# The query projection of a decoder block as a Strassen step, with streamed weight sums

## The chip, the cores and the metric

The kernel runs on one core of a Trainium2 chip. Its engines work beside one another, each with its own list of instructions, done in order: TensorE (PE in the profile; PEld is its loading of weights), VectorE (DVE), ScalarE (ACT), GpSimd (POOL) and SyncE (SP), whose list here is nearly all of the kernel's DMA issues. The metric is the device time of one execution in microseconds (us).

## The reference

One decoder block on `x` of 1024 tokens by 1024 features, in fp32. A mixer with two branches comes first, then cross-attention to 256 memory tokens (4 heads of 256), then a SwiGLU network with 2816 inner features. The change touches the middle:

```
merged = sigmoid(g_ssd) * (y_ssd @ w_up_ssd) + sigmoid(g_gla) * (y_gla @ w_up_gla)
h = x + merged @ w_o
q = rmsnorm(h, norm_xattn) @ w_xq                   # 1024 x 1024 times 1024 x 1024
s = q_h @ k_h.T * 256**-0.5;  p = softmax(s);  o_h = p @ v_h      # 4 heads
h = h + o @ w_xo
g, u = split(rmsnorm(h, norm_ffn) @ w_ffn_in)
out = rmsnorm(h + (silu(g) * u) @ w_ffn_out, norm_final)
```

## The kernel before, in words

Each fp32 factor of a large product is split into a rounded part and a remainder (`split`, lines 226 to 228: ACT copies the first, DVE subtracts it to get the second), and TensorE makes three products of them. One matmul takes a 128x128 block of the left factor and 512 columns of the right one.

Stages follow each other: the input projection and the two branches, `dense(0)` (w_up_ssd), `dense(1)` (w_up_gla), `dense(2)` (w_o), `dense(3)` (w_xq), attention, `dense(4)` (w_xo), the two products with w_ffn_in, and the one with w_ffn_out. A `dense` makes 16 chains of 24 matmuls, one for each block of 128 output features (o) and half of the tokens (j). `Left` fetches weights in 1 MB pieces (`raw`) and splits them into `wd`, two chains ahead.

After each chain of `dense(2)`, `residual` adds x, stores the result `ga` in DRAM (`h1_d`), and `put_xq` makes the split operand `hl` of the next product: an ACT copy and a DVE instruction over 512 columns. `Stats` sums squares into `ssum`, by POOL or DVE, as `either` decides by a running estimate of both engines.

The products with w_ffn_in and w_ffn_out are Strassen-Winograd steps: both factors are cut into quarters, and seven products of quarters and of sums of quarters stand for eight. For w_ffn_out the sums of weights are made ahead: `presum` (line 1297) takes eleven blocks of 256 rows, one at a time through one buffer `pre`. For each it loads 1 MB, POOL makes four sums (one `sa<-pre`, then three into `pre`), and each is stored in `down_d`. All eleven are made beside `dense(0)` to `dense(2)`. The `run` helper (442) interleaves such side work with the chains.

Attention goes through eight units, two for each head. Keys and values of a head are loaded (`ga<-kT_d`, `ga<-vm_d`) and split into `kvhl` by ACT and DVE; in the loop scores of unit n, the transposes of unit n-1 (`bank<-ident,pe`, then `phl`) and the products with the values of unit n-2 (`bank<-phl,kvhl`, then `hl`) alternate.

Within an engine the order is not that of the program alone: a scheduler with a model of the engines' times fills each engine's list, within data dependences and priorities (`ahead()` raises one). An instruction handed to `pinned` (132) keeps its place in the program's order instead.

Of the kernel before, what the change touches and what calls it, by code (L numbers as in the profile page):

```python
# [9 lines left out]
F32 = mybir.dt.float32  # L10
# [6 lines left out]
P = 128  # L17
# [61 lines left out]
def block_kernel(ctx: ExitStack, tc: tile.TileContext, t: dict, out: bass.AP):  # L79
# [19 lines left out]
    def dram(name, *shape):  # L99
        return dr.tile(list(shape), F32, name=name, tag=name)  # L100
# [16 lines left out]
    down_d = dram("down_d", 4 * D_FF // 2, HALF)  # L117
    kT_d = dram("kT_d", D, MEM)
# [1070 lines left out]

    class Left:  # L1190
# [30 lines left out]
    left = Left((t["w_up_ssd"], t["w_up_gla"], t["w_o"], t["w_xq"], t["w_xo"]))  # L1221
# [34 lines left out]
    i_ys, i_yg, i_wo, i_xq, i_q, i_xo = (paired(x) for x in (EVEN, ODD, EVEN, ODD, EVEN, EVEN))  # L1256
# [40 lines left out]
    def presum():  # L1297


        r = slot("m", (P, 2, D), name="pre")  # L1300
        for k in range(KP):
            SP.dma_start(r, t["w_ffn_out"][256 * k:256 * k + 256, :].rearrange("(j p) c -> p j c", p=P))
# [3 lines left out]
            put = lambda n, ap: SP.dma_start(down_d[(n * KP + k) * P:(n * KP + k + 1) * P, :], ap)  # L1306
# [73 lines left out]
    run(dense(2, i_wo, residual(h1_d, s1, "norm_xattn", put_xq, 0.5), quad_of(xT_d)), (early, 1.1))  # L1380
# [3 lines left out]

    def load_kv(h):
        es = [rp.tile([P, 2, 256], F32, name="ga", tag="ga") for _ in range(2)]
        h_ = slot("m" if h < 3 else "op", (P, 2, 4, 256), F32R, name="kvhl")
        SP.dma_start(es[0], kT_d[h * 256:(h + 1) * 256, :].rearrange("(i p) m -> p i m", p=P))
        SP.dma_start(es[1], vm_d[:, h * 256:(h + 1) * 256].rearrange("(i p) c -> p i c", p=P))
        for i in range(2):  # L1390
            split(es[i], h_[:, 0, 2 * i:2 * i + 2], h_[:, 1, 2 * i:2 * i + 2])
        kv.append(h_)
# [144 lines left out]
    for n, _ in enumerate(dense(4, i_xo, residual(h2_d, u_xo_stats, "norm_ffn", put_xo), quad_of(h1_d), js=(1, 0))):  # L1537
# [213 lines left out]
```

## Time and profile before

Three runs took 1947.55 to 1952.03 us, their median is 1949.75. The profile is of one execution:

| | |
|---|---|
| span of the profiled execution | 1949.0 us |
| median of the runs | 1949.75 us |
| PE busy (matmuls) | 1916.2 us, 98% of the span |
| DVE busy | 1298.5 us, 67% |
| ACT busy | 845.8 us, 43% |
| POOL busy | 557.8 us, 29% |

By the matmuls' names in the timeline w_o runs from about 985 to 1074 us, the query projection to 1156, attention to 1217, w_xo to 1305. PE is hardly ever idle, so the busy time of others costs something only where PE waits for it.

### The profile page before, as it was taken

The numbers are of one execution on the slowest core, as the hardware profiler recorded it, in microseconds if no ns is written. First come the engines' busy times: TensorE is split into PE (matmuls) and PEld (weight loads), VectorE is DVE, ScalarE is ACT, GpSimd is POOL, SyncE is SP. The second block draws the span as 40 slices with busy tenths as digits, with TensorE's granted clock in tenths as the row PEclk, the third lists the DMA queues.
The fourth block names the chain that finished last, engine by engine and source line by source line (L and its number), as shares of the span: only waits on it lengthen the run. The fifth ranks groups of instructions, "written<-read, shape, count | busy, mean of one in ns | idle before, by whom it ended". The sixth has DMA issues, their size and how long they took to land.

```text
span 1949.0 us, 26264 instructions
## 1 busy us (share of the span) xinstructions
PE 1916.2 (98%) x9776; PEld 1615.6 (83%) x9776; DVE 1298.5 (67%) x1873; ACT 845.8 (43%) x1485; POOL 557.8 (29%) x428
## 2 busy tenths in 40 slices
PE   7999999999999999999999999999999999999998
PEld 7998787888878888788887888888888888888888
DVE  7766879877776764655534237677777777766566
ACT  7534564655553444643223235444333333345243
POOL 0012334345543231022433000006445544320002
PEclk9999999999999999999999999999999999999999
DMA  9423383446553653997675201442233224177463
GB/s 341 144 93 101 130 307 107 152 161 186 174 173 123 198 167 124 348 346 270 226 269 164 82 22 44 140 141 82 90 126 110 82 100 144 42 271 239 157 224 126
DMA packets 237875, 317.98 MB, mean 163 GB/s; under 512 B 16538, under 2 KB 156036, under 8 KB 237748
## 3 DMA queue, kind: packets, MB, share of 16 engines
q1 hardware_dynamic: 236020, 310.01, 47.4%
q10 hardware_dynamic: 1728, 6.29, 0.8%
q8 instruction: 77, 1.26, 0.3%
q14 instruction: 50, 0.41, 0.1%
HBM read 215.27 MB, written 100.99 MB: 162 GB/s over the span
## 4 chain that ended last, share of the span: by engine, by line
PE 43%; DMA 3%; POOL 2%; DVE 1%; issue 1%; ACT 1%; POOLq 0%; SPq 0%; DVEq 0%; ACTq 0%
PE acc L51 38%; PE bank L51 4%; DMA pre<-in_w_ffn_out_dram 1%; POOL pre L73 1%; DMA down_d<-pre 1%; PE bank L55 1%; POOL ssum L73 0%; DVE hl L73 0%; POOL sa L73 0%; DMA h_d<-ga 0%; DMA ga<-vm_d 0%; DVE wd L73 0%; ACT wd L227 0%; ACT sq L493 0%; DVE phl L73 0%
## 5 line engine op out<-in xcount | busy, mean ns | idle before, releaser
L51 PE MATMUL acc<-hl,wd 128*128 128x512 f32 x1920 | 440.4, 390 | 3.6 <-DVE wd L73 2.0
L51 PEld LDWEIGHTS acc<-hl,wd 128*128 128x128 f32 x1920 | 359.6, 188 | 80.7 <-DVE wd L73 3.3
L73 DVE TENSOR_TENSOR wlo<-raw,whi 128x512 fp32r<-128x512 f32 x272 | 236.4, 875 | 103.6 <-ACT whi L227 103.5
L227 ACT ACTIVATE whi<-raw 128x512 fp32r<-128x512 f32 x272 | 169.5, 629 | 247.6 <-PE acc L51 201.0
L73 DVE TENSOR_TENSOR o<-acc,o 128x512 f32<-128x512 f32 (+1 forms) x256 | 172.6, 676 | 108.8 <-PE acc L51 95.4
L51 PE MATMUL acc<-fs 128*128 128x512 f32 (+1 forms) x792 | 155.7, 356 | 0.1
L51 PEld LDWEIGHTS acc<-fs 128*128 128x128 f32 x792 | 130.7, 189 | 20.8 <-issue 0.5
L73 DVE TENSOR_TENSOR fs<-fr,fs 128x1024 fp32r<-128x1024 f32 (+1 forms) x84 | 98.9, 1217 | 36.5 <-ACT fs L227 36.4
L227 ACT ACTIVATE fs<-fr 128x1024 fp32r<-128x1024 f32 (+1 forms) x84 | 79.2, 982 | 95.9 <-PE acc L51 31.2
L73 POOL TENSOR_TENSOR raw<-raw,sa 128x512 f32<-128x512 f32 x44 | 57.1, 1297 | 207.8 <-DVE wlo L73 207.8
L73 POOL TENSOR_TENSOR sa<-raw 128x512 f32<-128x512 f32 x43 | 69.6, 1619 | 107.0 <-DMA raw<-in_w_in_dram 78.9
L227 ACT ACTIVATE whi<-sa 128x512 fp32r<-128x512 f32 x96 | 59.6, 626 | 93.7 <-PE acc L51 92.3
L73 DVE TENSOR_TENSOR wlo<-sa,whi 128x512 fp32r<-128x512 f32 x96 | 80.9, 843 | 13.7 <-ACT whi L227 12.7
L73 DVE TENSOR_TENSOR wd<-raw,wd 128x1024 fp32r<-128x1024 f32 x40 | 52.8, 1323 | 47.6 <-ACT wd L227 47.2
L73 POOL TENSOR_TENSOR rstd<-rstd,mhalf 128x4 f32<-128x4 f32 (+1 forms) x7 | 8.7, 1246 | 257.0 <-DVE rstd L73 257.0
L227 ACT ACTIVATE wd<-raw 128x1024 fp32r<-128x1024 f32 x40 | 42.2, 1057 | 90.4 <-PE acc L51 89.8
L51 PE MATMUL acc<-T4h,whi 128*128 128x512 f32 x192 | 76.3, 397 | 2.4 <-DVE o L73 2.4
L51 PE MATMUL acc<-B22h,wlo 128*128 128x512 f32 x192 | 75.7, 394 | 1.5 <-DVE wlo L73 1.5
L51 PE MATMUL acc<-T1h,whi 128*128 128x512 f32 x192 | 76.3, 397 | 0.0
L51 PE MATMUL acc<-T2h,whi 128*128 128x512 f32 x192 | 75.9, 395 | 0.0
L51 PE MATMUL acc<-T3h,whi 128*128 128x512 f32 x192 | 75.9, 395 | 0.0
L51 PE MATMUL acc<-B22h,whi 128*128 128x512 f32 x192 | 75.7, 394 | 0.0
(399 smaller groups left out, 4698.6 us busy)
## 6 DMA issues: line engine op xcount, KB each, us to landing
raw<-in_w_in_dram SPq DMA_DIRECT2D x26, 1024.0 KB, 5.9
raw<-in_w_ffn_in_dram SPq DMA_DIRECT2D x22, 1024.0 KB, 6.5
act_d<-o SPq DMA_DIRECT2D x77, 256.0 KB, 2.1
fr<-act_d SPq DMA_DIRECT2D x35, 512.0 KB, 7.9
pre<-in_w_ffn_out_dram SPq DMA_DIRECT2D x11, 1024.0 KB, 10.0
fr<-down_d SPq DMA_DIRECT2D x20, 512.0 KB, 3.9
down_d<-pre SPq DMA_DIRECT2D x33, 256.0 KB, 3.1
h_d<-ga SPq DMA_DIRECT2D x32, 256.0 KB, 3.1
```

What stands on the lines that cost most here:

```text
L51: return s.e.matmul(o, x, y, **kw)
L55: return s.e.transpose(o, x, i)
L73: return f(*a, **kw)
L227: ACT.activation(hi, src, AF.Copy)
```

## The change

A class `Wide` makes the query projection as one Strassen-Winograd step: seven products of 512x512 quarters, each in two halves of the inner dimension (`kp`), so 14 steps of 24 matmuls. Weights come as 1 MB tiles `wr` in the order of the products: three quarters of `w_xq` itself, and four sums of quarters from `xqs_d`. These sums are made by `presum`, which now takes four blocks of `w_xq` and the first four of `w_ffn_out` beside `dense(0)` to `dense(2)`; the other seven of `w_ffn_out` (`late`) are made in steps between the units of attention and the chains of w_xo. `put_xq` is one ACT copy into fp32 quarters `rq`; their sums are made by DVE during the projection, and split there (`ws`). Products are taken up by ACT copies and DVE adds into `wk`, and finished quarters are split into the operands of attention. Keys and values of heads 0 and 1 are loaded during the projection, those of heads 2 and 3 during attention; the loads of `wr` and of keys and values are pinned. The first pieces of `w_xo` come during the projection.

```diff
+    class Wide:
...
+        SEQ = ("B11", "T1", "B22", "T2", "B21", "T3", "T4")
+        LEFT = {"B11": (0, 0), "B21": (0, 1), "T1": 0, "B22": 3, "T2": 1, "T3": 2, "T4": (1, 1)}
+        COMB = {"T1": ((0, 0), (0, 1), (0, 0)), "T2": ((0, 0), (1, 1), (0, 0)), "T3": ((0, 1), (1, 1), (0, 1)),
+                "T4": ((1, 0), (1, 0), (0, 0))}
+        RIGHT = {"B11": (0, 0), "B22": (1, 1), "B21": (1, 0), "T1": (0, 0), "T2": (0, 0), "T3": (0, 1), "T4": (1, 0)}
+        OUT = {"B11": (0, 0), "T1": (1, 1), "B22": (0, 1), "T2": (0, 1), "B21": (0, 0), "T3": (1, 1), "T4": (1, 0)}
...
+        def load(s, n):
+            while len(s.raw) < min(n, 7):
+                src = s.LEFT[s.SEQ[len(s.raw)]]
+                if isinstance(src, tuple):
+                    i, j = src
+                    w = s.W[half(j), half(i)]
+                else:
+                    w = s.sums_d[half(src), :]
+                r = slot(s.keys[len(s.raw)], (P, 4, HALF), name="wr")
+                pinned(SP.dma_start(r, w.rearrange("(k p) c -> p k c", p=P)))
+                s.raw.append(r)
...
+        def prep(s, n):
+            while len(s.ops) < min(n, 14):
+                m, kp = divmod(len(s.ops), 2)
+                s.load(m + 1)
+                name, c = s.SEQ[m], slice(2 * kp, 2 * kp + 2)
+                x = [slot("op", (P, 2, 2, HALF), F32R, name="ws") for _ in range(2)]
+                with ahead():
+                    if name in s.COMB:
+                        o, a, b = (s.quad(*ij)[:, c] for ij in s.COMB[name])
+                        sub(s.two(o), o, a, b)
+                    split(s.raw[m][:, c], x[0][:, 0], x[0][:, 1])
+                    split(s.quad(*s.RIGHT[name])[:, c], x[1][:, 0], x[1][:, 1])
+                s.ops.append(x)
...
+        def evac(s, name, u, p):
+            i, j = s.OUT[name]
+            o = p if name == "T4" and s.base is None else s.home(i, j)[:, u]
+            first = name in ("B11", "T1", "B22")
+            with ahead():
+                if s.base is not None:
+                    DVE.scalar_tensor_tensor(o, p, s.scale, o, ALU.mult, ALU.add)
+                elif first:
+                    ACT.activation(o, p, AF.Copy)
+                elif name != "T4":
+                    add(DVE, o, p, o)
+                if not first:
+                    s.post(i, j, u, o)
...
+        def steps(s):
+            x = 0
+            for m, name in enumerate(s.SEQ):
+                if name in ("B11", "T1", "B21"):
+                    banks = [(acc if name == "B11" else bank)() for _ in range(4)]
+                    if name == "B11":
+                        s.chain = banks
+                elif name in ("T2", "T3", "T4"):
+                    banks = s.chain
+                fresh = name in ("B11", "T1", "B21")
+                if s.base is not None:
+                    s.home(*s.OUT[name])
+                for kp in range(2):
+                    s.load(m + 3)
+                    s.prep(x + 3)
+                    w, b = s.ops[x]
+                    for u in range(4):
+                        for k in range(2):
+                            for n, (a, c) in enumerate(((0, 0), (0, 1), (1, 0))):
+                                PE.matmul(banks[u], w[:, a, k, u * P:(u + 1) * P], b[:, c, k],
+                                          start=fresh and kp + k + n == 0, stop=kp + k == 2 and n == 2,
+                                          skip_group_check=True)
+                    x += 1
+                    if kp:
+                        for u in range(4):
+                            s.evac(name, u, banks[u])
+                    yield
...
-    left = Left((t["w_up_ssd"], t["w_up_gla"], t["w_o"], t["w_xq"], t["w_xo"]))
+    left = Left((t["w_up_ssd"], t["w_up_gla"], t["w_o"], t["w_xo"]))
...
+    wides = (("w_xq", xqs_d), )
+
+    def presum(part, key):
+
+
+        todo = [(t[w].rearrange("(j k p) c -> k p j c", j=2, p=P)[k], d, 4, k) for w, d in wides for k in range(4)]
+        todo += [(t["w_ffn_out"][256 * k:256 * k + 256, :].rearrange("(j p) c -> p j c", p=P), down_d, KP, k)
+                 for k in range(KP)]
+        r = slot(key, (P, 2, D), name="pre")
+        for src, dst, kn, k in todo[part]:
+            SP.dma_start(r, src)
...
+    xq = Wide(t["w_xq"], xqs_d, lambda i, j, u, p: into(i_q, 4 * i + u, j, p), ("aux", "op", "aux") * 3, ("aux",) * 3)
+
     def put_xq(o, j, q, g):
-        x = hl(i_xq, o)
-        h, l = x[:, 0, half(j)], x[:, 1, half(j)]
-        ACT.activation(h, q, AF.Copy, scale=g)
-        DVE.scalar_tensor_tensor(l, q, g, h, ALU.mult, ALU.subtract)
+        ACT.activation(xq.quad(o // 4, j)[:, o % 4], q, AF.Copy, scale=g)
...
-    early = presum()
+    early = presum(slice(0, 8), "m")
...
+    run(dense(2, i_wo, residual(h1_d, s1, "norm_xattn", put_xq, 0.5), quad_of(xT_d)), (early, 1.3))
+    drain(early)
...
+    def fetch_kv(h):
+        es = [rp.tile([P, 2, 256], F32, name="ga", tag="ga") for _ in range(2)]
+        pinned(SP.dma_start(es[0], kT_d[h * 256:(h + 1) * 256, :].rearrange("(i p) m -> p i m", p=P)))
+        pinned(SP.dma_start(es[1], vm_d[:, h * 256:(h + 1) * 256].rearrange("(i p) c -> p i c", p=P)))
+        return es
+
+    def split_kv(es, pin=lambda x: x):
+        h_ = slot("op" if kv else "m", (P, 2, 4, 256), F32R, name="kvhl")
+        for i in range(2):
+            pin(ACT.activation(h_[:, 0, 2 * i:2 * i + 2], es[i], AF.Copy))
+            pin(sub(DVE, h_[:, 1, 2 * i:2 * i + 2], es[i], h_[:, 0, 2 * i:2 * i + 2]))
+        kv.append(h_)
...
-    run(dense(3, i_xq, lambda o, j, p, g: into(i_q, o, j, p)), (xq_side(), 1.0), (early, 1.0))
-    drain(early)
-    load_kv(0)
+    def kv_side():
+        for _ in range(2):
+            yield
+        es = fetch_kv(0)
+        for _ in range(9):
+            yield
+        split_kv(es, pinned)
+        yield
+
+    def next_left():
+        left.limit = len(left.seq)
+        left.upto(26)
+        yield
+
+    run(xq.steps(), (xq_side(), 1.0), (kv_side(), 1.0), (waiting(next_left(), 12), 1.0))
...
+    late = presum(slice(8, None), "op")
...
+        for _ in range(3):
+            next(late, None)
...
+    for n, _ in enumerate(dense(3, i_xo, residual(h2_d, u_xo_stats, "norm_ffn", put_xo), quad_of(h1_d), js=(1, 0))):
+        for _ in range(1):
+            next(late, None)
```

Counts of the two programs: 9267 matmuls before and 9219 now (384 of the old projection go, 336 come). POOL makes 11 blocks of weight sums before and 15 now; of the sums of squares `ssum` POOL makes 22 before and 8 now, DVE 23 and 37. DVE's 16 `hl<-ga,cols,hl` go.

The first place is SP's list at the end of w_o. Before, `ga_9338` is the result of the last chain of w_o, and `raw_9299` the second piece of w_xq (the first, `raw_9145`, stands 13 rows ahead of it):

```order
L1360 DMA h1_d_67<-ga_8882 128x512 [waits DMAHW6_49,DVE_49]
L1201 DMA raw_9299<-in_w_xq_dram 128x8x256 [waits DMAHW7_49,DVE_49]
L1184 DMA ga_9107<-xT_d_66 128x512 [waits DMAHW6_49,DVE_49,Activation_49]
...
L1360 DMA h1_d_67<-ga_9301 128x512 [waits DVE_49]
L1184 DMA ga_10631<-h1_d_67 128x512 [waits DMAHW5_49,DVE_49,Activation_49]
L1360 DMA h1_d_67<-ga_9338 128x512 [waits DVE_49]
L1201 DMA raw_9448<-in_w_xq_dram 128x8x256 [waits DMAHW0_49,DVE_49]
```

Now the last chain's result is `ga_9323`, and the first three tiles of the projection are `wr_9429`, `wr_9431` and `wr_9433`:

```order
L1464 DMA h1_d_67<-ga_9251 128x512 [waits DMAHW3_49,DVE_49]
L1464 DMA h1_d_67<-ga_9287 128x512 [waits DVE_49]
L1464 DMA h1_d_67<-ga_9323 128x512 [waits DMAHW5_49,DVE_49]
L1222 DMA wr_9429<-in_w_xq_dram 128x4x512
L1222 DMA wr_9431<-xqs_d_82 128x4x512 [waits DMAHW7_49]
L1222 DMA wr_9433<-xqs_d_82 128x4x512 [waits DMAHW0_49]
```

Before, two of the four pieces of w_xq were issued among the stores of the first chains; now every tile of w_xq stands behind the store of the last chain's result, which waits for DVE. The load of `wr_9429` has no wait of its own.

The second place is DVE's list at the same boundary, now (`acc_9393` is the last chain of w_o, `ws_9435` the first left operand of the projection):

```order
L73 SCALAR_TENSOR_TENSOR ga_9323<-acc_9393,ga_9323 128x512 [waits DMAHW7_49,DMAHW6_49,PE_49]
L73 TENSOR_TENSOR ssum_7620<-ssum_7620,sq_9421 128x512 [waits Activation_49]
L73 TENSOR_TENSOR ws_9435<-wr_9429,ws_9435 128x1024 [waits DMAHW6_49,Activation_49]
L73 TENSOR_TENSOR ws_9436<-rq_8876,ws_9436 128x1024 [waits Activation_49]
L73 TENSOR_TENSOR ws_9441<-wr_9429,ws_9441 128x1024 [waits Activation_49]
```

and before (`acc_9411` the last chain, `wd_7628` a left operand of the projection):

```order
L73 TENSOR_TENSOR wd_7575<-raw_9145,wd_7575 128x1024 [waits Activation_49]
L73 SCALAR_TENSOR_TENSOR hl_9330<-ga_9261,cols_120,hl_9330 128x512 [waits Activation_49]
L73 SCALAR_TENSOR_TENSOR ga_9301<-acc_9375,ga_9301 128x512 [waits PE_49]
L73 SCALAR_TENSOR_TENSOR hl_9402<-ga_9301,cols_120,hl_9402 128x512 [waits Activation_49]
L73 SCALAR_TENSOR_TENSOR ga_9338<-acc_9411,ga_9338 128x512 [waits DMAHW7_49,DMAHW0_49,PE_49]
L73 TENSOR_TENSOR wd_7628<-raw_9145,wd_7628 128x1024 [waits Activation_49]
```

The first left operands of the projection stood around the last chain's result; now they stand behind it and wait for a DMA.

The third place is the middle of attention. On SP (`pre` loads are the first blocks of `late`, `ga_10288` and `ga_10289` the keys and values of head 3), now:

```order
L1406 DMA pre_10038<-in_w_ffn_out_dram 128x2x1024 [waits DMAHW4_49,PE_49]
...
L1406 DMA pre_10038<-in_w_ffn_out_dram 128x2x1024 [waits DMAHW6_49,DMAHW7_49,DMAHW1_49,DMAHW0_49]
...
L1406 DMA pre_10038<-in_w_ffn_out_dram 128x2x1024 [waits DMAHW7_49,DMAHW6_49,DMAHW5_49]
L1410 DMA down_d_81<-sa_10285 128x512 [waits Pool_49]
L1491 DMA ga_10288<-kT_d_83 128x2x256 [waits DMAHW2_49,DVE_49]
L1492 DMA ga_10289<-vm_d_84 128x2x256 [waits DMAHW3_49,DVE_49]
```

and on ACT, the splits of that head among those of earlier units (`hl` and `phl` are operands of w_xo and of the products with the values):

```order
L228 ACTIVATE phl_10171<-bank_10142 128x512
L1498 ACTIVATE kvhl_10292<-ga_10288 128x512 [waits DMAHW2_49]
L1498 ACTIVATE kvhl_10292<-ga_10289 128x512 [waits DMAHW3_49]
L228 ACTIVATE hl_10154<-bank_10233 128x512 [waits PE_49]
L228 ACTIVATE hl_10164<-bank_10242 128x512 [waits PE_49]
L228 ACTIVATE phl_10255<-bank_10227 128x512 [waits DVE_49]
```

Before, keys and values of all heads stood ahead of the last store of w_o on SP. Now those of head 3 stand behind the first sum of the third late block, and the ACT splits `hl_10154` and `phl_10255` behind the split of head 3.

## Rows read from the trace of the kernel before

**Rows 1.** Windows: busy us by engine (PE, PEld, DVE, ACT, POOL), PEclk, DMA share, GB/s.

```profile
985.00:1074.00 89.00, 86.93 (x380) 70.70 (x380) 41.24 (x44) 29.80 (x44) 35.48 (x26) 1.00 0.63 210
...
1162.00:1217.00 55.00, 54.61 (x339) 47.96 (x338) 41.34 (x108) 34.81 (x94) 0.00 (x0) 1.00 0.12 39
```

**Rows 2.** Chain that ended last, in order of time: start, length, what.

```profile
1184.53 3.71 PE acc L51 x31
...
1204.70 0.87 PE bank L55 x8
...
1212.37 2.76 PE bank L51 x12
...
1320.48 459.26 PE acc L51 x2026
```

**Rows 3.** Timeline of PE, w_o: start, length, work; in brackets idle time before, its releaser.

```profile
1033.34 21.60 PE L51 MATMUL acc<-hl,wd 128*128 128x512 f32 x94 [0.76 <-DVE wd L73]
...
1056.60 17.97 PE L51 MATMUL acc<-hl,wd 128*128 128x512 f32 x78 [0.78 <-DVE wd L73]
1074.73 9.36 PE L51 MATMUL acc<-hl,wd 128*128 128x512 f32 x40 [0.15 <-DVE hl L73]
```

**Rows 4.** Timeline of DVE and SP, end of w_o.

```profile
1054.73 0.68 DVE L73 SCALAR_TENSOR_TENSOR ga<-acc,ga 128x512 f32<-128x512 f32 x1
...
1055.44 0.33 SPq L1360 DMA_DIRECT2D h_d<-ga  x1
...
1073.36 0.42 SPq L1360 DMA_DIRECT2D h_d<-ga  x1
```

**Rows 5.** The page's DMA issues: KB each, median us from issue to landing.

```profile
raw<-in_w_in_dram SPq DMA_DIRECT2D x26, 1024.0 KB, 5.9
...
pre<-in_w_ffn_out_dram SPq DMA_DIRECT2D x11, 1024.0 KB, 10.0
```

**Rows 6.** Chain of waits, 965 to 1010 us: the presum's blocks.

```profile
971.21 1.29 POOL sa L73
...
979.91 4.84 DMA pre<-in_w_ffn_out_dram
...
984.92 1.29 POOL sa L73
...
1005.82 1.28 POOL sa L73
```

**Rows 7.** Tile raw: engine, operation, ns min/median/max of one.

```profile
L227 ACT ACTIVATE wd<-raw x40: 1039/1061/1065, 800.8 to 1275.2; 128x1024 fp32r<-128x1024 f32 x40
L73 DVE TENSOR_TENSOR wd<-raw,wd x40: 1211/1225/2319, 803.2 to 1276.3; 128x1024 fp32r<-128x1024 f32 x40
```

**Rows 8.** Windows as in group 1, around a fall of the clock.

```profile
50.00:55.00 5.00, 3.26 (x27) 3.06 (x26) 5.00 (x9) 1.94 (x5) 0.00 (x0) 1.00 1.08 375
55.00:60.00 5.00, 5.00 (x30) 4.78 (x29) 5.00 (x9) 2.56 (x5) 0.00 (x0) 0.66 0.34 123
```

**Rows 9.** Chain of waits, 1026 to 1076 us: loads of keys and values.

```profile
1050.76 2.67 DMA ga<-kT_d
...
1054.84 3.04 DMA ga<-vm_d
```

**Rows 10.** Timeline, attention: its first matmuls, and the split of a head.

```profile
1156.50 7.96 PE L51 MATMUL acc<-kvhl,hl 128*128 128x256 f32 x65
...
1174.26 1.23 ACT L227 ACTIVATE kvhl<-ga 128x512 fp32r<-128x512 f32 x2
```

**Rows 11.** Tile pre: POOL's sums, ns min/median/max of one.

```profile
L73 POOL TENSOR_TENSOR pre<-pre x22: 1272/1733/2359, 836.6 to 1025.6; 128x512 f32<-128x512 f32 x22
...
L73 POOL TENSOR_TENSOR sa<-pre x11: 1278/1287/2158, 834.0 to 1021.8; 128x512 f32<-128x512 f32 x11
L73 POOL TENSOR_TENSOR pre<-sa,pre x11: 1282/1298/1637, 835.3 to 1023.1; 128x512 f32<-128x512 f32 x11
```

**Rows 12.** Tile S: a DVE operation with operands in SBUF, ns min/median/max.

```profile
L73 DVE TENSOR_SCALAR S<-S,ebl x32: 340/348/1443, 639.8 to 768.0; 128x256 f32<-128x256 f32 x32
```

More of the change, by code (lines that the diff above doesn't have):

```diff
@@ L117, in block_kernel @@
     down_d = dram("down_d", 4 * D_FF // 2, HALF)
+    xqs_d = dram("xqs_d", 2 * D, HALF)
     kT_d = dram("kT_d", D, MEM)
@@ L1188, in block_kernel, with __init__, quad, home @@
     JS = (0, 1)
+    class Wide:
[5 more added lines that the diff above has]
+        OUT = {"B11": (0, 0), "T1": (1, 1), "B22": (0, 1), "T2": (0, 1), "B21": (0, 0), "T3": (1, 1), "T4": (1, 0)}
+        def __init__(s, W, sums_d, post, keys, side, base=None, scale=1.0, two=None):
+            s.W, s.sums_d, s.post, s.keys, s.side, s.base, s.scale = W, sums_d, post, keys, side, base, scale
+            s.two = two or (lambda ap: DVE)
+            s.q, s.raw, s.ops, s.keep, s.chain = {}, [], [], {}, None
+        def quad(s, i, j):
+            if (i, j) not in s.q:
+                s.q[i, j] = slot("op", (P, 4, HALF), name="rq")
+            return s.q[i, j]
+        def load(s, n):
[9 more added lines that the diff above has]
+                s.raw.append(r)
+        def home(s, i, j):
+            if (i, j) not in s.keep:
+                k = s.keep[i, j] = slot(s.side[len(s.keep)], (P, 4, HALF), name="wk")
+                if s.base is not None:
+                    pinned(SP.dma_start(k, s.base[half(i), half(j)].rearrange("(u p) c -> p u c", p=P)))
+            return s.keep[i, j]
+        def prep(s, n):
[34 more added lines that the diff above has]
+                fresh = name in ("B11", "T1", "B21")
+                if s.base is not None:
+                    s.home(*s.OUT[name])
[14 more added lines that the diff above has]
+                    yield
@@ L1195, in __init__ @@
             s.seq, s.raw, s.w, s.ring = [(W, u) for W in mats for u in range(4)], [], [], []
+            s.limit = 12
         def load(s, n):
-            while len(s.raw) < min(n, len(s.seq)):
+            while len(s.raw) < min(n, s.limit):
                 W, u = s.seq[len(s.raw)]
@@ L1204, in upto @@
         def upto(s, n):
-            while len(s.w) < min(n, 2 * len(s.seq)):
+            while len(s.w) < min(n, 2 * s.limit):
                 u, i = divmod(len(s.w), 2)
@@ L1255, in block_kernel @@
     EVEN, ODD = ("op",) * 8, ("op",) * 6 + ("aux",) * 2
-    i_ys, i_yg, i_wo, i_xq, i_q, i_xo = (paired(x) for x in (EVEN, ODD, EVEN, ODD, EVEN, EVEN))
+    i_ys, i_yg, i_wo, i_q, i_xo = (paired(x) for x in (EVEN, ODD, EVEN, EVEN, EVEN))
     def fetch(src, dst, gain=None):
@@ L1295, in block_kernel @@
     s1 = Stats(rp)
[L1297 to L1302, printed above, removed]
+    wides = (("w_xq", xqs_d), )
[6 more added lines that the diff above has]
+            SP.dma_start(r, src)
             yield
@@ L1305, in presum @@
             s1_ = sums["m"].tile([P, HALF], F32, name="sa", tag="sa", bufs=2)
[L1306 removed]
+            put = lambda n, ap: SP.dma_start(dst[(n * kn + k) * P:(n * kn + k + 1) * P, :], ap)
             add(POOL, s1_, a(1, 0), a(1, 1))
@@ L1375, in waiting @@
             yield
-    early = presum()
+    early = presum(slice(0, 8), "m")
     run(dense(0, i_ys, post_ys, lambda o, j: gate(gs_d, o, j)), (fetch_gated(yg_d, sr_d, i_yg), 1.0), (waiting(early, 12), 1.0))
     run(dense(1, i_yg, post_yg, lambda o, j: (gate(gg_d, o, j), quad(ysg_d, o * P, 0, j))), (early, 1.1))
-    run(dense(2, i_wo, residual(h1_d, s1, "norm_xattn", put_xq, 0.5), quad_of(xT_d)), (early, 1.1))
+    run(dense(2, i_wo, residual(h1_d, s1, "norm_xattn", put_xq, 0.5), quad_of(xT_d)), (early, 1.3))
+    drain(early)
     kv = []
-    def load_kv(h):
[L1386 to L1392, printed above, removed]
+    def fetch_kv(h):
[9 more added lines that the diff above has]
+        kv.append(h_)
+    def load_kv(h):
+        split_kv(fetch_kv(h))
     xsc = cp.tile([P, NCH], F32, name="xsc")
```

1 line of the change is left out of this document (removed).

## The prediction

> **What bounds the kernel now.** I read the windows first, since a busy share over the whole span says little of one stage. During w_o PE is busy 86.93 of 89.00 us, during attention 54.61 of 55.00, at full clock in both [rows 1]. So PE's work is the time, and a change is worth its matmuls less the waits that it puts between them. The chain of waits gives the rate: 459.26 us for 2026 matmuls over 512 columns, 0.2267 us each [rows 2]. PE's timeline then shows where the 2.07 us of idle time in w_o lie: 0.76 and 0.78 us are waits for DVE's weight splits, and at the border to the projection PE waits 0.15 us [rows 3]. This border is nearly seamless because the first pieces of w_xq come early. POOL is busy 35.48 us in w_o and not at all in attention, the DMA queues 0.63 and 0.12 of the time [rows 1]: the work that moves leaves a stage with little room for one with much.
>
> **The matmuls.** 384 go and 336 come, of the same shape: 48 x 0.2267 = **10.9 us saved**. The 14 steps keep PE's rate if their operands are there.
>
> **The entry to the projection.** Now the first tile `wr_9429` stands on SP behind the store of the last result of w_o, though its load waits for nothing itself. Let T0 be the end of w_o's last matmul. DVE makes the result in 0.68 us, the store starts 0.03 later and occupies SP 0.42 [rows 4], so the load is issued at T0 + 1.1. A load of 1 MB lands 5.9 us after its issue in the median of those during the input projection, 4.84 in a quiet stretch, 10.0 in the median of the presum's [rows 5, 6]. I take 5.9, since only the last stores and the two next tiles move then: T0 + 7.0. Behind that ACT copies twice at 1.061 us (weight tile, then the activation quarter, which has long been ready but stands behind in ACT's list), so until 9.1; DVE subtracts twice at 1.225 us [rows 7], from 8.1 to 10.5. PE has four matmuls that need the copies alone (0.9 us) and then waits for the second remainder. Idle: 10.5 - 0.9 = 9.6, in place of 0.15: **+9.5 us**, with 8.5 and 13.6 at the other two landings. Queued behind are all of PE's 336 matmuls, so nothing covers it.
>
> The clock adds to it. Between 50 and 55 us PE was busy for 3.26 of 5 us, and in the next 5 us the granted clock was 0.66 [rows 8]: part of that stretch ran at 1.2 GHz instead of 2.4, and 0.34 x 5 = 1.7 us of PE's full-speed work were lost. A gap of 9.6 us is emptier than that. I take **+1.7**, bounds 0 (the waits of 0.8 us in w_o, which left 1.00 granted) and 1.7.
> The Trainium skill ("TensorE: Matmul & The Clock Gate", Part 1: The HAM clock gate) says that the throttled state is the default and activity releases it; by that rule the projection starts at half clock and the 1.7 stand, by the waits of w_o alone it would be 0.
>
> **w_o itself.** The splits of PE's weights were late there by 0.76 and 0.78 us [rows 3]. DVE loses 16 instructions for `hl`, SP the eight loads of keys and values; DVE gains sums of squares from POOL, 14 in all. I take the two waits as gone: **-1.5 us**, bounds 0 and -2.07 (all the idle time of the stage).
>
> **Inside the projection.** A step is 24 x 0.2267 = 5.4 us of PE. DVE has for it two splits (2.45 us) and in 8 of 14 steps a subtraction over 128x1024 (1.2), besides evacuations over 512 columns at about 0.68: some 64 us of 76. Laid out in the order of its list this leaves PE fed; the closest place is T3 to T4, with under 1 us to spare. I take **0**, bounds 0 and 3. The eight subtractions and the quarter copies cost nothing while DVE has those 12 us; a DVE instruction that is held up shows as PE idle at T4.
>
> **Attention.** The late blocks make SP's list a chain: load, POOL's sums, stores, next load; the loads for head 3 stand behind the first sum of the third block. Let A be the start of attention. The first `pre` waits for PE's last T3 matmul, 48 x 0.2267 = 10.9 before A. It lands 4.84 later, first sum about A - 5.9. From one first sum to the next it took 984.92 - 971.21 = 13.71 us in a quiet stretch, 1005.82 - 984.92 = 20.90 in a crowded one [rows 6]. I take 13.71 (DMA share 0.12 in attention [rows 1]): the third block's first sum begins at A + 21.5 and ends at 22.8, keys are issued at 23.2, values 0.4 later; with 2.67 and 3.04 us to land [rows 9] they are there at 25.9 and 26.6. ACT, at 0.62 us a copy [rows 10], and DVE, at 0.68, then do in list order the split of head 3, `hl_10154`, `hl_10164` and `phl_10255`, whose remainder is ready at A + 29.7. PE's work up to the matmul that needs it: 144 over 256 columns at 3.71/31, 32 transposes at 0.87/8, 24 at 2.76/12 [rows 2] = 17.2 + 3.5 + 5.5 = 26.2. **+3.5 us**; 0 if the keys are there by A + 22, 10.7 if one of the two blocks ahead takes 20.90. Before, ACT finished the comparable split at 1175.5, 19 us into attention [rows 10], so without the chain on SP nothing would wait.
>
> **w_xo and the rest.** Blocks 4 to 7 of `late` stand beside w_xo; DVE and ACT are no nearer to PE there than in the dense stages above, and w_ffn_out needs their sums only some 400 us later: **0**.
>
> **Sum.** -10.9 + 9.5 + 1.7 - 1.5 + 0 + 3.5 = +2.3 on the profiled span of 1949.0: 1951.3. The median of the runs lies 0.75 above that span, so I forecast 1952.0 us. Less than 0.2% either way, 3.9 us (1945.9 to 1953.7), is what a measurement of this kernel cannot tell from no change; the forecast is no change.
>
> **Rivals.**
> *Head 3 is in time.* If the third block is two or three us earlier, or ACT reaches these splits later anyway, the 3.5 us go: 1948.5. For it: the margin is 3.5 us out of a chain of 37 (A - 10.9 to A + 26.6). Against it: the chain on SP has no slack, and 13.71 is the shortest cycle in the rows.
> *A short entry.* The load lands in 4.84, the clock holds, w_o loses all of its idle time, head 3 is in time: -10.9 + 8.5 - 2.07 = -4.5, so 1945.3. For it: the queues are nearly empty at that moment. Against it: four conditions at once.
> *POOL is slow beside attention, and slower comes out.* POOL's sums took 1.29 to 1.73 us in the median and up to 2.16, 1.64 and 2.36 [rows 11], DVE's short operation on SBUF 0.35 and up to 1.44 [rows 12]: sometimes one held up the other. In attention DVE is busy 41.34 of 55 us [rows 1]. With all sums at their longest a block takes 2.16 + 1.64 + 2 x 2.36 = 8.5 us of POOL in place of 5.9, so two blocks and the first sum of the third are late by 2 x 2.6 + 0.9 = 6.1 us, and all of this lands on the wait for head 3: 1952.0 + 6.1 = 1958.1. It decides as soon as the keys land after A + 22. For it: DVE's share. Against it: most of DVE's attention work reads PSUM on one side, and in w_o POOL was near its shortest.
> The Trainium skill ("SBUF — State Buffer", Who interferes with whom) has a rule for this: a DVE instruction with two SBUF inputs and a GpSimd one that reads SBUF share a port pair that one holds for a whole instruction; by it each sum pays for such neighbours, and the 1958.1 stand; by the medians of the rows they would not.
>
> **How the numbers follow.** Forecast 0.48 (own range 1948 to 1956), head 3 in time 0.20, short entry 0.12, slow POOL 0.20. The forecast lies close under the upper bound of no change, so its share is split 0.28 same, 0.20 slower. With the others: faster 0.12, same 0.48, slower 0.40. The range 1945 to 1960 takes in the short entry, the longest landing at the entry (+4.1, 1956) and the slow POOL.
>
> **What would show it.** In the changed profile: PE's work on `ws,ws` in 336 matmuls; a wait of 9 to 10 us before the first of them, released by DVE `ws`, with `wr` on the chain of waits and a granted clock under 1.00 behind it; no wait for `wd` over 0.5 us in w_o; a wait of 2 to 5 us before `bank<-phl,kvhl` or the transposes next to it, in the second half of attention, with `pre`, `sa` and `kT_d` on the chain; PE without gaps over 1 us inside the projection and in w_xo. The entry being under 6 us would break the forecast most, and waits inside the projection, in T2 to T4, next.

## The result, and the profile after

The changed kernel takes 1952.98 us (median of ten runs, 1951.08 to 1954.95), the kernel before 1947.36 in its ten runs beside it: ratio 1.0029, 95% interval 1.0020 to 1.0039. So it is slower by 5.6 us in the medians. The profiled execution spans 1950.7 us, against 1949.0 before.

These two spans differ by 1.7 us only because of a part that the change doesn't touch. Up to the first matmul of w_up_ssd the engines' lists are alike, and yet here it starts 3.3 us sooner. PE's timeline, first before (this matmul, and the second one of the FFN), then now:

```profile
801.93 2.14 PE L51 MATMUL acc<-hl,wd 128*128 128x512 f32 x8 [0.98 <-ACT wd L227]
...
1297.25 0.39 PE L51 MATMUL acc<-B11l,whi 128*128 128x512 f32 x1
```

```profile
798.65 2.14 PE L51 MATMUL acc<-hl,wd 128*128 128x512 f32 x8 [0.69 <-ACT wd L228]
...
1070.00 9.42 PE L51 MATMUL acc<-ws 128*128 128x512 f32 x28 [9.18 <-ACT ws L228]
...
1150.91 7.12 PE L51 MATMUL acc<-kvhl,hl 128*128 128x256 f32 x58
...
1163.17 0.44 PE L55 MATMUL bank<-ident,pe 128*128 128x128 f32 x2 [0.62 <-DVE pe L73]
...
1165.84 3.01 PE L51 MATMUL bank<-phl,kvhl 128*128 128x512 f32 x12 [0.70 <-DVE phl L73]
...
1176.02 1.40 PE L51 MATMUL bank<-phl,kvhl 128*128 128x512 f32 x5 [0.36 <-DVE phl L73]
...
1179.73 0.66 PE L55 MATMUL bank<-ident,pe 128*128 128x128 f32 x4 [0.58 <-DVE hl L73]
1180.56 0.66 PE L55 MATMUL bank<-ident,pe 128*128 128x128 f32 x4 [0.17 <-DVE hl L73]
...
1192.49 3.02 PE L51 MATMUL bank<-phl,kvhl 128*128 128x512 f32 x12 [1.69 <-DVE phl L73]
...
1196.92 0.66 PE L55 MATMUL bank<-ident,pe 128*128 128x128 f32 x4 [0.72 <-DVE hl L73]
...
1232.89 66.00 PE L51 MATMUL acc<-hl,wd 128*128 128x512 f32 x288 [0.47 <-ACT wd L228]
...
1298.95 0.39 PE L51 MATMUL acc<-B11l,whi 128*128 128x512 f32 x1
```

One thing in the account of the kernel before needs a correction: the matmuls of w_o and of the old projection have the same names, so the border at 1074 us can't be read off them. Counted, PE starts 1184 matmuls from 801.93 to 1074.73 us, and the three stages up to w_o have 1152. So 32 matmuls of the old projection (7.3 us) stand among the last ones of w_o, and cover the time in which its last results are made.

The reader is to see three things. The waits for `wd` in w_o [rows 3] are gone. Before the first `ws` matmul PE stands for 9.18 us. And in attention there are seven waits, 4.84 us in sum, all of them released by DVE. From w_up_ssd to the start of attention the changed kernel takes 352.3 us where before it was 354.6 (1156.50 - 801.93): 2.3 less. From there to the end of w_xo, taken here and below at the second matmul of the FFN, it takes 148.0 us (1298.95 - 1150.91), where the kernel before took 140.8: 7.3 more. Together +5.0, near the 5.6 of the medians.

The windows of the changed kernel (columns as in [rows 1]: PE, PEld, DVE, ACT, POOL, granted clock, DMA share, GB/s) show w_o, the wait, the projection's start, its rest, and attention:

```profile
971.00:1061.00 90.00, 89.82 (x397) 74.06 (x395) 30.51 (x40) 26.10 (x38) 3.37 (x3) 1.00 0.36 122
1061.00:1070.00 9.00, 0.00 (x1) 0.00 (x1) 2.21 (x3) 3.30 (x5) 0.00 (x0) 0.76 0.82 283
1070.00:1076.00 6.00, 6.00 (x14) 4.75 (x15) 6.00 (x7) 4.79 (x5) 0.00 (x0) 0.50 1.06 387
1076.00:1151.00 75.00, 75.00 (x340) 62.36 (x340) 56.60 (x66) 40.95 (x56) 7.09 (x6) 1.00 0.35 118
1151.00:1206.00 55.00, 50.02 (x326) 43.95 (x325) 49.59 (x102) 32.58 (x91) 20.54 (x16) 1.00 0.58 202
```

The clock fell while PE stood, and the first 6.0 us of the projection ran at 1.2 GHz: 14 matmuls in 6.0 us, 3.0 us lost. In the first 55 us of attention DVE is busy 49.59 us, before 42.67 (the window of [rows 1], with 41.34, begins 5.5 us into attention), though its list there is nearly the same, and POOL 20.54 in place of 0.

The chain of waits around the wait at the entry has the prediction's steps one by one:

```profile
1060.86 0.70 DVE ga L73
...
1061.58 0.32 SPq L1464
...
1061.95 5.97 DMA wr<-in_w_xq_dram
...
1067.94 2.01 ACT ws L228 x2
...
1070.00 9.42 PE acc L51 x28
```

The store of w_o's last result, then the first tile's load (5.97 us to land, 5.9 forecast), then ACT's two copies.

### The profile page after: what moved, and what is told of

Read it like the earlier page. It is cut to its first block, busy times and chain, and to the rows that moved or that the text cites. A ratio compares the mean times of both kernels' runs of the same rounds, so it can differ in the third digit from the quotient of the medians.

```text
span 1950.7 us, 26279 instructions
## 1 busy us (share of the span) xinstructions
PE 1907.9 (98%) x9728; PEld 1608.3 (82%) x9728; DVE 1343.2 (69%) x1911; ACT 872.6 (45%) x1517; POOL 557.0 (29%) x430
## 4 chain that ended last, share of the span: by engine, by line
PE 85%; DVE 8%; issue 2%; DMA 2%; ACT 2%; POOL 0%; SPq 0%; POOLq 0%; DVEq 0%; ACTq 0%
PE acc L51 70%; PE bank L51 13%; DVE cv L73 2%; DVE wlo L73 2%; PE bank L55 1%; DVE hs L73 1%; DVE o L73 1%; DMA zr<-sz_d 1%; DVE pe L73 1%; DMA hl<-ys_d 0%; DVE mx L73 0%; POOL ssum L73 0%; ACT cv L753 0%; DMA wr<-in_w_xq_dram 0%; DMA sz_d<-zr 0%
## 5 line engine op out<-in xcount | busy, mean ns | idle before, releaser
L51 PE MATMUL acc<-hl,wd 128*128 128x512 f32 x1536 | 350.9, 390 | 1.6 <-ACT wd L228 1.2
L51 PEld LDWEIGHTS acc<-hl,wd 128*128 128x128 f32 x1536 | 287.6, 188 | 63.2 <-ACT wd L228 2.4
L73 POOL TENSOR_TENSOR raw<-raw,sa 128x512 f32<-128x512 f32 x44 | 57.1, 1297 | 209.2 <-DVE wlo L73 209.2
L73 POOL TENSOR_TENSOR sa<-pre 128x512 f32<-128x512 f32 x15 | 19.4, 1292 | 223.1 <-DMA pre<-in_w_xq_dram 93.2
L51 PE MATMUL acc<-T2l,whi 128*128 128x512 f32 x192 | 75.2, 392 | 0.0
```

Source lines behind the costliest of these rows:

```text
L51: return s.e.matmul(o, x, y, **kw)
L73: return f(*a, **kw)
```

## The experiments

All are against the kernel before on the same chip. Beside the experiments that kernel's median was 1947.78 to 1948.46 us, beside the changed kernel 1947.36, so a difference of one microsecond between an experiment's median and the changed kernel's 1952.98 says nothing by itself. The sections are read as the time from one matmul to another in PE's timeline, which leaves out the chance of the earlier stages.

**First loads early.**

```diff
+    def first_wr():
+        xq.load(2)
+        yield
-    run(dense(2, ...), (early, 1.3))
+    run(dense(2, ...), (early, 1.3), (waiting(first_wr(), 10), 1.0))
```

> Of the changed kernel, only the place of the first two wr loads differs: they are issued inside w_o, from its eleventh chain on, instead of behind its last store. Entry theory: the wait of 9.2 us before the first ws matmul is the load's latency alone, and the half clock behind it (10.2 us, 6.0 of them with PE at work, so 3.0 us lost) is caused by that wait. Then the wait falls under 1.5 us, the clock stays at 1.00, and the time falls by 8.5 to 12.2 us against the changed kernel's 1953.0: 1941 to 1944, ratio to before 0.997 to 0.998. Rival, that the wait turns up again elsewhere (DVE's work of 64 in 76 us inside the projection is the bound, and the wait gave it a lead): the wait at the entry goes, but waits of 5 us or more for DVE appear inside the projection, and the time falls by less than 5 us (1948 or more).

Measured: 1941.23 us, ratio 0.9962 (0.9950 to 0.9975), 11.7 us below the changed kernel. PE goes from w_o into the projection without a wait, and the windows show the clock at 1.00:

```profile
1061.00:1064.00 3.00, 3.00 (x15) 2.47 (x14) 3.00 (x4) 3.00 (x4) 0.00 (x0) 1.00 0.03 5
1064.00:1070.00 6.00, 6.00 (x28) 4.97 (x27) 6.00 (x6) 2.62 (x5) 0.00 (x0) 1.00 0.53 166
```

Attention and w_xo take the same 148.0 us, and from w_up_ssd to attention it takes 340.0 us in place of 352.3. So 9.2 + 3.0 us were, in the profiled execution, the price of a load that waited for nothing but its place in the list, and the wait gave DVE no lead that the projection needed.

**PE kept busy at the entry** (44 matmuls into a bank that nobody reads, ahead of the projection):

```diff
+            d = bank()
+            for k in range(44):
+                PE.matmul(d, i_wo[7][:, 0, :P], i_wo[7][:, 0, half(0)], start=True, stop=True)
```

> To the changed kernel 44 matmuls of 512 columns into an unused bank are added between w_o and the projection (10.0 us at 0.2267 us each), their result is not used. The load still lands when it did. Clock theory: the half clock comes from PE's idle time at the entry; with PE at work the granted clock stays 1.00 and the first 6 us of the projection run at full speed: 3.0 us less, minus up to 1 us by which the added work outlasts the wait: 1950 to 1951. Rival, that the half clock has another cause (the 16 DMA engines at full share, the change of operands): it stays, and the time is 1953 to 1954.

Measured: 1952.24 us, 1.0018 (1.0009 to 1.0027). PE's timeline, and the windows of the same stretch:

```profile
1063.63 10.13 PE L51 MATMUL bank<-hl 128*128 128x512 f32 x44
1073.85 1.21 PE L51 MATMUL acc<-ws 128*128 128x512 f32 x4
1075.30 5.74 PE L51 MATMUL acc<-ws 128*128 128x512 f32 x24 [0.23 <-DVE ws L73]
```

```profile
1070.00:1072.00 2.00, 2.00 (x10) 1.67 (x9) 0.00 (x0) 0.21 (x1) 0.00 (x0) 1.00 1.01 365
1072.00:1074.00 2.00, 1.92 (x9) 1.28 (x8) 1.12 (x1) 2.00 (x3) 0.00 (x0) 1.00 1.06 407
```

With the DMA engines as full as before and the same loads, the clock stays at 1.00: PE's standing still is what lowers it. The projection from its first matmul on takes 78.7 us in place of 80.9. Of the 3.0 us some 1 goes to the added work outlasting the wait. The median, 0.7 us lower, is above the 1950 to 1951 of the clock theory and not clear of the runs' spread; the clock itself is the evidence.

**Keys and values one head earlier** (heads 2 and 3 are loaded when head 1 and head 2 are split):

```diff
-            load_kv(a.h + 1)
+            while len(got_kv) < min(a.h + 3, 4):
+                got_kv.append(fetch_kv(len(got_kv)))
+            split_kv(got_kv[a.h + 1])
```

> Of the changed kernel, only the loads of keys and values of heads 2 and 3 move: each is issued one head earlier on SP, so that head 3 no longer stands behind the third late block. The POOL sums stay. Chain theory (the prediction's): the waits in the middle of attention come from the split of head 3, which waits for its load; they go, 3 to 3.5 us: 1949.5. Hold-up theory: PE waits in attention because POOL's sums hold up DVE's scaling of pe (x32, up to 1.46 us each in place of 0.35), and the split of head 3 only adds its own waiting of 1 us or less: the waits before transposes and value products stay at 4 us or more in sum, the time falls by 0 to 1.5 us: 1951.5 to 1953.

Measured: 1950.27 us, 1.0013 (1.0004 to 1.0022). Attention and w_xo take 143.8 us, 4.2 less, and the first 40 us of the FFN 3.1 more, in a profiled execution that took 1953.58 us, 3.3 over the median. By the expectation this speaks for the chain on SP. But the trace shows that the edit also moved POOL's bursts: DVE's 32 scalings of `pe` take 10.9 us in sum here and 20.5 in the changed kernel. The experiment changed both suspects and decides nothing by itself.

**No POOL sums in attention** (the four POOL instructions of a late block work on 8 of 512 columns; most sums of the seven blocks are left out, their loads and stores stay):

```diff
+            w = HALF if key == "m" else 8
-            add(POOL, s1_, a(1, 0), a(1, 1))
+            add(POOL, s1_[:, :w], a(1, 0)[:, :w], a(1, 1)[:, :w])
...
```

> Of the changed kernel, the POOL instructions of the seven late blocks are cut to 8 of 512 columns each; their loads and stores stay, so most sums of those blocks are left out. Hold-up theory: DVE's scaling of pe stays at 0.34 to 0.36 us each, the waits of attention, also those before 1167 us that stand ahead of head 3's load, go, and the time falls by 5 to 6.5 us: 1946.5 to 1948. Chain theory: the chain on SP is shorter by two blocks of POOL (about 11 us), so head 3 is in time and its part of the waits goes, 3 to 3.5 us: 1949.5, but the waits before 1167 us (0.6 and 0.7 listed) stay.

Measured: 1948.6 us, 1.0006 (0.9998 to 1.0015). Attention and w_xo 144.0 us, 4.0 less, and the waits before 1167 us are gone, which stood ahead of anything of head 3. The scalings of `pe` in the groups of instructions over attention, first of the kernel before, then of the changed kernel, then of this one (busy us, mean ns of one, idle before):

```profile
L73 DVE TENSOR_SCALAR pe<-pe,sm 128x256 f32<-128x256 f32 x32 | 9.9, 348 | 0.2
```

```profile
L73 DVE TENSOR_SCALAR pe<-pe,sm 128x256 f32<-128x256 f32 x32 | 20.5, 681 | 0.3
```

```profile
L73 DVE TENSOR_SCALAR pe<-pe,sm 128x256 f32<-128x256 f32 x32 | 9.8, 348 | 0.2
```

Without POOL's sums each scaling is back at 348 ns. The time lies between the two forecasts and decides nothing by itself; the scalings and the early waits do. But the edit also brings the keys of head 3 forward, to 14.7 us into attention from 20.8, so a part of the 4.0 us could still be theirs.

**The same with each late block loaded twice** (a second, equal load behind each):

```diff
             SP.dma_start(r, src)
+            if key == "op":
+                SP.dma_start(r, src)
```

> As the third experiment (POOL's instructions of the late blocks cut to 8 columns, most of these sums left out), but each late block is loaded twice, one load after the other, so that the chain on SP ahead of head 3's keys is about as long as in the changed kernel (5 us more of DMA a block in place of about 6 us of POOL). Chain theory: the waits in the middle of attention come back, 3 us or more against the third experiment's 1948.6: 1951.5 to 1953. Hold-up theory: no POOL work beside DVE, so the time stays within 1 us of the third experiment: 1948 to 1949.5, with the scaling of pe at 0.34 to 0.36 us.

Measured: 1953.7 us, 1.0034 (1.0021 to 1.0047); attention and w_xo 146.8 us, 2.8 more than with single loads. The chain can hurt, as the chain theory says. But it was not "about as long" as in the changed kernel: here the keys of head 3 are issued 29.1 us into attention (1181.04 - 1151.96), there 20.8, as SP's timeline shows for this kernel and the changed one:

```profile
1181.04 0.38 SPq L1495 DMA_DIRECT2D ga<-kT_d  x1
```

```profile
1171.74 0.38 SPq L1491 DMA_DIRECT2D ga<-kT_d  x1
```

So it prices a delay of 8 us more than the change has, and leaves open what the real one costs.

**Scaling on ACT.** This leaves POOL's sums and the chain on SP alone and takes DVE's part in the collision away:

```diff
-                DVE.tensor_scalar(s.e[:, 2 * a2 + a], s.e[:, 2 * a2 + a], sm[:, a:a + 1], None, ALU.mult)
+                ACT.activation(s.e[:, 2 * a2 + a], s.e[:, 2 * a2 + a], AF.Copy, scale=sm[:, a:a + 1])
```

> Of the changed kernel, only the 32 scalings of pe by the reciprocal row sums move from DVE to ACT (ACT's copies of 128x256 with a scale: some 0.55 us each, 17.6 us on an engine that was busy 34.8 of 55 us in attention before). POOL's sums and head 3's place on SP stay. Hold-up theory: DVE loses 20.5 us of held-up work, the waits of attention fall to about 1.5 us, 1947 to 1949. Chain theory: the waits in the middle stay, 1950 or more. Rival to both: ACT is now late with exponentials and operand copies, PE waits for ACT, and the time is 1953 or more.

Measured: 1950.53 us, 1.0016 (1.0007 to 1.0025). The keys of head 3 are issued 21.6 us into attention, even later than in the changed kernel, and yet the stretch from the start of attention to the matmul that began at 1229 us in the changed kernel is 5.4 us shorter. PE's timeline has two waits left there, and two at w_xo, where there was one of 0.47 us:

```profile
1165.71 3.01 PE L51 MATMUL bank<-phl,kvhl 128*128 128x512 f32 x12 [0.64 <-DVE phl L73]
...
1179.23 0.66 PE L55 MATMUL bank<-ident,pe 128*128 128x128 f32 x4 [0.54 <-DVE hl L73]
...
1228.55 2.14 PE L51 MATMUL acc<-hl,wd 128*128 128x512 f32 x8 [0.80 <-ACT wd L228]
1231.61 63.78 PE L51 MATMUL acc<-hl,wd 128*128 128x512 f32 x280 [0.92 <-DVE wd L73]
```

Attention and w_xo take 143.8 us, 4.2 less than in the changed kernel, with head 3 as late as there: its keys cost at most the 0.5 us of the second row. The edit takes all scalings off DVE, not only what was held of them, so it bounds the chain on SP and doesn't price the collision by itself. The experiment without POOL's sums, in which the scalings stay on DVE, does: 4.0 us, less at most that 0.5. By its time alone, 1950.53, the expectation would speak for the chain theory ("1950 or more"), because something is given back: ACT's scalings take 517 ns each, the weight splits of w_xo are late (1.2 us), and the first 40 us of the FFN take 1.1 more.

**Eleven blocks early, four beside w_xo**, with the first loads early (rates of the side work raised to fit them in):

```diff
-    early = presum(slice(0, 8), "m")
+    early = presum(slice(0, 11), "m")
-    late = presum(slice(8, None), "op")
+    late = presum(slice(11, None), "op")
-        for _ in range(3):
-            next(late, None)
...
-        for _ in range(1):
+        for _ in range(2):
             next(late, None)
```

> The first experiment's early loads, and eleven blocks of sums (four of w_xq, seven of w_ffn_out) beside the three dense stages instead of eight; the last four beside w_xo, none beside attention. If attention's 4.8 to 6.5 us of extra PE waits come from work that the late blocks bring there (either theory), they go: 1941.2 - 5 = 1936. Rival: the blocks cost as much beside w_o or w_xo (DVE's weight splits held up there, or the first tiles of the FFN loaded late behind the stores on SP): then waits of 3 us or more appear in those stages and the time stays at 1940 to 1942.

Measured: 1946.83 us, 0.9995 (0.9986 to 1.0004): 5.6 us above the first experiment. Attention and w_xo take 145.6 us, 2.4 less than there, but the first 40 us of the FFN take 49.1 in place of 41.2. Attention was not free of POOL's work either: the scheduler put the first of the four late blocks into it, and three pairs of scalings were held there (1.65, 2.51 and 1.46 us). POOL's timeline and DVE's in attention:

```profile
1170.91 1.33 POOL L73 TENSOR_TENSOR sa<-pre 128x512 f32<-128x512 f32 x1 [68.42 <-DVE mx L73]
```

```profile
1172.57 2.51 DVE L73 TENSOR_SCALAR pe<-pe,sm 128x256 f32<-128x256 f32 x2
```

So what attention would take with no sums beside it, this experiment doesn't show. At the FFN's start ACT and DVE stand until the second weight tile lands:

```profile
1286.48 0.63 ACT L228 ACTIVATE whi<-raw 128x512 fp32r<-128x512 f32 x1 [5.59 <-DMA raw<-in_w_ffn_in_dram]
```

```profile
1286.48 0.69 DVE L73 TENSOR_TENSOR sa<-raw 128x512 f32<-128x512 f32 x1 [4.06 <-DMA raw<-in_w_ffn_in_dram]
```

SP issued this load at 1280.50 us, 6.1 ahead of the FFN's first matmul; in the first experiment it was 10.7 ahead. From then on ACT and DVE are behind. PE's timeline and the windows there:

```profile
1297.24 0.50 PE L51 MATMUL acc<-T1h,whi 128*128 128x512 f32 x1 [1.54 <-ACT whi L228]
1298.76 0.79 PE L51 MATMUL acc<-B21h,whi 128*128 128x512 f32 x1 [0.69 <-ACT whi L228]
1301.22 1.84 PE L51 MATMUL bank<-ones,ssum 128*128 128x1 f32 x8 [1.24 <-DVE ssum L73]
```

```profile
1292.00:1297.00 5.00, 3.70 (x21) 3.11 (x19) 5.00 (x10) 5.00 (x10) 0.00 (x0) 1.00 0.29 107
1297.00:1303.00 6.00, 3.83 (x13) 2.61 (x13) 6.00 (x11) 3.86 (x8) 0.00 (x0) 0.56 0.96 319
1303.00:1309.00 6.00, 6.00 (x17) 4.75 (x17) 6.00 (x13) 1.26 (x2) 2.96 (x2) 0.59 0.24 77
```

DVE is busy without a gap, and PE waits 1.54 us. Then the clock falls: in windows of 1 us it is 1.00 up to 1297, 0.87 in the next and 0.50 behind it, so the other two waits came after the fall. The three waits are 3.5 of the 7.9 us, and most of the rest is the half clock. The rival in the expectation was right in kind: the FFN's weights came late. Why SP issued them late (in its waits stand the landings of w_xo's stores, 7 us in two) was not separated further.

**Versions.** Four combinations with the first loads early: scalings on ACT; keys earlier; both; and half of the scalings on ACT, for which the edit is

```diff
+                if a:
+                    ACT.activation(s.e[:, 2 * a2 + a], s.e[:, 2 * a2 + a], AF.Copy, scale=sm[:, a:a + 1])
+                else:
                     DVE.tensor_scalar(s.e[:, 2 * a2 + a], s.e[:, 2 * a2 + a], sm[:, a:a + 1], None, ALU.mult)
```

> The first experiment's early loads together with the scalings on ACT. If the two causes are independent, their gains add: 11.7 us for the loads and what the scalings on ACT give alone: by the hold-up theory 1941.2 - 4 to 6 = 1935 to 1937, by the chain theory 1941 with attention's waits unchanged.

Measured: 1937.8 us, 0.9948 (0.9935 to 0.9962), 3.4 us below early loads alone: of the hold-up's 4 to 6 us a little less, with 2.6 us of waits for `wd` at w_xo.

> The first experiment's early loads together with the second's earlier keys and values, all scalings on DVE. In the second experiment only one of the scalings was held up, since POOL's bursts of about 6 us every 12 to 13 us fell beside other work of DVE, and 3.1 us were lost again at the entry of the FFN. Hold-up theory: what is gained in attention depends on where the bursts fall; with 1 to 2 held scalings attention and w_xo take 144 us, with five or six 148 us. Time 1941.2 - 0 to 4 = 1937 to 1941, plus up to 3 us if the FFN's entry is late as there.

Measured: 1939.4 us, 0.9956 (0.9941 to 0.9972), the scalings 10.8 us in sum and attention with w_xo 145.1 us, 1.1 above what was expected; the FFN's entry was in time.

> All three: early loads, keys and values one head earlier, scalings on ACT. Neither a held-up scaling nor head 3 can be late; what is left is ACT's added work, seen as 2.6 us of waits for wd at the start of w_xo in the experiment with early loads and scalings on ACT (1937.8). I expect the same within 1.5 us: 1936.5 to 1939; if the chain on SP had still cost something there, 1 us or more below 1937.

Measured: 1938.47 us, 0.9948 (0.9932 to 0.9963): earlier keys add nothing to scalings on ACT, so the chain on SP costs nothing that can be seen there.

> Early loads, and every second scaling on ACT, the others on DVE. Hold-up theory: half as many scalings can be held, and ACT has 8.8 us less to do than with all of them, so the waits for wd at the start of w_xo shrink below 1.5 us: attention and w_xo 144 to 146 us, the time 1937 to 1939.5. If holding up is a matter of single coincidences rather than of the count, the time can lie anywhere up to 1941.

Measured: 1937.18 us, 0.9945 (0.9931 to 0.9958), attention with w_xo 144.6 us. Not to be told apart from all scalings on ACT. This version beats the kernel before by 0.5% and the changed one by 0.8%.

## Why the prediction was right, and where not

It forecast 1952.0 us and no change as the likeliest; measured were 1952.98, and a ratio just clear of no change on the slow side, on which it had put 0.40. That the two times lie within 1 us of each other is in part luck. The forecast was 2.3 us on a base of 1949.75, the median of three runs; in the ten runs beside the result the base was 1947.36. So the change itself is 5.6 us (5.0 by the timelines) where 2.3 was forecast. The terms, one by one:

- *The matmuls.* 48 fewer, at the same rate: right.
- *The entry.* 9.5 us forecast, 9.0 measured (9.18 less 0.15): right, and by its own steps, but for the last. PE was released by ACT's `ws` and not DVE's; the second remainder was ready at 1071.4 us, before PE, at half clock, needed it. In the four other profiles of kernels whose lists are the same up to there (keys and values earlier, no sums, double loads, scaling on ACT) the wait was 8.5 to 9.4 us.
- *The clock.* 1.7 us forecast, 3.0 measured in the profiled execution. The mechanism held. The size differs from one execution to the next: PE's list in the projection is the same in those four profiles, and from its first `ws` matmul to attention it takes 80.9 us in the changed kernel and 80.3, 80.2, 79.7 and 81.0 in them, against 78.0 with the clock at 1.00 in the first experiment. So the half clock cost 1.7 to 3.0 us. The forecast is the low end of this, and its upper bound was wrong: the only row [rows 8] was a short fall with PE at work through most of it.
- *w_o.* 1.5 us forecast; the three waits of before there (0.38, 0.76 and 0.78) are all gone, 1.9 of listed idle time. That understates them: from 804.50 to 1074.73 us PE started 1176 matmuls before, 266.6 us at 0.2267 each, in 270.2, so these waits and the border cost 3.6. Counted in this way the entry is 9.4 now, and the terms up to attention, -10.9 + 9.4 + 3.0 - 3.6 = -2.1, meet the 2.3 less of the timelines.
- *Inside the projection.* No wait forecast, none measured; DVE was busy 56.60 of its last 75 us.
- *Attention.* 3.5 us forecast, 4.84 in listed waits and 7.3 between the two kernels from its start to the end of w_xo. Here a step failed: the wait was put on head 3's keys, landing 25.9 us into attention. They landed at 23.7, since a late block took 12.2 to 12.5 us in place of 13.71, and by the prediction's own sum that leaves some 1.3 us (3.5 less 2.2); the scaling on ACT bounds it at about 0.5. No single wait of 2 us or more came, as the prediction's signs had it; the largest was 1.69. And the chain of waits from 1155 to 1200 us has four pairs of scalings on it (2.35, 1.71, 2.68 and 2.23 us), and neither `pre`, `sa` nor `kT_d`. What happened instead is on DVE's timeline and POOL's, in the changed kernel:

```profile
1158.23 2.35 DVE L73 TENSOR_SCALAR pe<-pe,sm 128x256 f32<-128x256 f32 x2
...
1161.67 1.71 DVE L73 TENSOR_SCALAR pe<-pe,sm 128x256 f32<-128x256 f32 x2
...
1171.35 2.76 DVE L73 TENSOR_SCALAR pe<-pe,sm 128x256 f32<-128x256 f32 x2
...
1188.29 2.31 DVE L73 TENSOR_SCALAR pe<-pe,sm 128x256 f32<-128x256 f32 x2
```

```profile
1157.77 1.29 POOL L73 TENSOR_TENSOR sa<-pre 128x512 f32<-128x512 f32 x1 [7.29 <-issue]
...
1160.39 2.58 POOL L73 TENSOR_TENSOR pre<-pre 128x512 f32<-128x512 f32 x2
...
1170.00 1.30 POOL L73 TENSOR_TENSOR sa<-pre 128x512 f32<-128x512 f32 x1 [7.03 <-issue]
...
1172.62 2.63 POOL L73 TENSOR_TENSOR pre<-pre 128x512 f32<-128x512 f32 x2
...
1187.80 1.29 POOL L73 TENSOR_TENSOR sa<-pre 128x512 f32<-128x512 f32 x1 [12.55 <-DMA pre<-in_w_ffn_out_dram]
```

Two scalings take 0.61 us beside an idle POOL; these pairs, each begun inside a burst of four sums on POOL (5.2 us), take 1.7 to 2.8, and PE's waits at 1163, 1165, 1176 and 1192 us follow them. The rival of a slow POOL had the right collision and the wrong payer: POOL's sums kept close to their shortest time, 1.27 to 1.35 us in attention, and DVE waited. It had a chance of 0.20 and 1958.1 us, from a cost that went through SP; the one that counted went straight to PE, through the engine that had 41 to 43 of 55 us to do already.

The Trainium skill ("SBUF — State Buffer", Who interferes with whom) says that an instruction of DVE's in a mode with two ports and one of GpSimd's exclude each other for a whole instruction, and names tensor_scalar among those that can enter such a mode. The trace agrees: the 11 scalings that met a sum took 949 to 1464 ns, the 21 others 341 to 355; the mode itself is in no row. The prediction weighed the other half of that rule, the instructions with two inputs in SBUF, and found few of them in attention; the row for the half that mattered was there [rows 12], 348 ns and up to 1443.

About 3 us of the 7.3 stay open. With the sums left out, attention and w_xo still take 144.0 us against 140.8, with two waits of 0.7 us for `hl` before transposes and one of 0.5 for `wd` that the kernel before doesn't have; the order of PE's list, the splits of keys inside attention and the last evacuations of the projection all differ there, and no run separates them.

## What to carry to other kernels

A load that waits for nothing can still be the latest thing in the kernel, by its place in a queue of stores: read the list around each stage border before counting matmuls, and price the gap with the clock that it costs behind it (here 8.5 to 9.4 us of standing and 1.7 to 3.0 lost at half clock, about what the 48 matmuls saved or more). When work goes to an idle engine, look first at which short instructions of another engine it holds up, and at how much room that engine has; a burst of 5.2 us that falls on them is paid by whoever waits for that engine. And a difference of two profiles is to be read from stage to stage: here 3.3 us of it came from stages that were the same in both.

## What was not expected of the hardware

The clock fell within the gap of 9.2 us and came back only after 6.0 us of dense matmuls at 1.2 GHz; with PE kept at work there it did not fall. One gap did not have one price: over five executions with gaps of 8.5 to 9.4 us the half clock cost 1.7 to 3.0.

While POOL made its sums beside attention, two kinds of DVE's instructions there were held, both with their operands in SBUF alone: the scalings of 128x256 (949 to 1464 ns in place of 348) and `mx<-mx,xsc` over 2 columns (533 to 1212 in place of 160). Beside the same sums instructions with an input in PSUM took their usual time, 670 to 693 ns over 512 columns, and so did the reciprocals over 2 columns, 151 to 166. The sums themselves stayed within 1.27 to 1.35 us.

A single wait of 1.5 to 1.8 us was enough in some executions to lower the clock: at the FFN's start with eleven blocks early (1.54 us, behind eight matmuls over one column), and at the start of w_xo in the version with all three edits (waits of 0.80 and 1.76, then 0.50 granted from 1223.3 to 1226.6 us). In the version with early loads and scalings on ACT nearly the same two waits, 0.80 and 1.79, left it at 1.00. So a small wait can cost more than its length, and whether it does is not fixed by the length alone.
